# A hybrid SGU and latent-attention trunk: rows scaled by their reciprocal norm on VectorE and turned by plain transposes, in place of products with a diagonal

## The chip, the cores and the metric

The kernel runs on one core of a Trainium2 chip. The metric is the device time of one execution in microseconds (us), as the median of several runs; the profile is of one execution. PE is TensorE, DVE is VectorE, ACT is ScalarE, POOL is GpSimd, SP is SyncE, whose queue issues nearly all loads.

## What is computed

Two layers over a residual stream x of 256 rows and 2048 columns, all float32. Each layer normalises the rows, modulates them by a scale and a shift that come from a condition vector c, runs a mixer, and adds the gated, normalised result:

```python
cond = jax.nn.silu(c)
for i in range(DEPTH):
    mod = cond @ ada_w[i] + ada_b[i]
    shift, scale, gate = jnp.split(mod, 3, axis=-1)
    h = rms_norm(x, pre_g[i]) * (1 + scale[:, None, :]) + shift[:, None, :]
    j = i // N_MIXERS
    if i % N_MIXERS == 0:
        y = sgu_mixer(h, sgu_w_in[j], sgu_norm_g[j], sgu_w_s[j], sgu_b_s[j], sgu_w_out[j])
    else:
        y = mla_mixer(h, mla_w_in[j], mla_q_norm_g[j], mla_kv_norm_g[j], mla_w_uq[j], mla_w_ukv[j], mla_w_out[j])
    x = x + gate[:, None, :] * rms_norm(y, post_g[i])
```

Layer 0's mixer projects h to 12288 columns (gelu, layer norm, a spatial product, a silu gate) and back; layer 1's is latent attention of 16 heads. The change concerns only how h is made: `rms_norm(x, ...)`, which multiplies each row of x by the reciprocal of its root mean square, and the turning of the rows, so that the columns of x lie on the partitions, as the projections need it.

## The kernel before

The 256 rows are two blocks (b = 0, 1) of 128 rows on the 128 partitions. Weights stream from HBM in granules of two row chunks of 128 by 512 columns (512 KB); each is split into a high part (a cast on ACT, L71) and a low part (a subtraction on DVE, L72), and a product is the sum of three: high by high, high by low, low by high. A granule makes 12 such 128x512 matmuls, 6 for each block.

**What sets the order.** The class `Stream` (L60) holds two lists: loads, and stages (splits of granules, and hooks for other work). `get` runs the stages until the splits are a few granules (2 to 4) ahead of the products; a load is issued on SP when its stage comes within `RAW_BUFS` = 6 items. The queues of all engines keep the order in which the program issues, so a hook stands in an engine's queue where the stream put it. `spread(main, extra)` (L134) lays the items of `extra` evenly between those of `main`: here adaLN's items (load, multiply and sum `ada_w`, L289; sums over the partitions on PE, L301; L309 to L313 give shift and scale) and the steps that turn h, between weight granules.

**Layer 0.** x lies in tiles `xn[b][q]`, 128 rows by 512 columns, q = 0 to 3. `norm_x` (L525) forms each row's reciprocal root mean square on DVE and makes a diagonal of it, `dg0[b]`, tile `dx` (`diag_of`, L264, a multiplication of the identity). `turn_hT(k)` (L428) turns two column chunks, k and k + 1, of both blocks by four products of x with the diagonal into a PSUM bank `ht`: the product turns the rows and scales them at once. Then ACT applies scale and shift (`hf`, L458) and casts (`hH`, L461), and DVE makes the low part (`hL`, L465). This happens in eight turns, k = 0, 2, ..., 14. The first stands among the hooks at the start; the others come from `hT_steps` (L450), a list of steps in which turning, modulating and the low part of consecutive turns follow each other one step apart. `STEPS` (L30) says before which visit of the first projection each group is wanted. A visit (product `pi`) sums one 512-column chunk over the row chunks known so far into a PSUM bank; there are four such banks, and they are evacuated by ACT (L662) or added by DVE (L669) one step later.

**Between the layers.** `ready1` (L877) adds the residual to block b and takes the sums of squares; its last step makes the diagonal `dg1[b]` (tile `d`). The order in which the two layers interlock is written out by hand in `PLAN` (L53): T, F, H, L with two digits turn, modulate, cast, and make the low part of block b's quarter q; s splits a granule of weights, g and b are products of block 0 and of block 1 (`pm`), e and c are what is left of layer 0. `turn_h1` (L920) is T: four products with the diagonal into two PSUM banks `h`, and `mod_h1` is F, half on ACT, half on DVE.

Of the kernel before, what the change touches and what calls it, by code (L numbers as in the profile page):

```python
# [8 lines left out]
F32 = mybir.dt.float32  # L9
# [6 lines left out]
P = 128  # L16
# [12 lines left out]
# chunks of adaLN's rows: (first, number, the first projection's visit before which they come)  # L29
STEPS = ((0, 2, 0), (2, 2, 24), (4, 2, 45), (6, 2, 78), (8, 4, 115), (12, 4, 162))  # L30
# how far the splitting of weights runs ahead of their products, and where other work lies between them
# [19 lines left out]
# from layer 0 to layer 1: T, F, H, L turn, modulate and split block b's quarter q; g, b are products of block 0 and  # L51
# of block 1, s splits weights, c and e are what is left of layer 0
PLAN = "e1 e1 e1 e1 T00 T01 s1 F00 F01 H00 L00 H01 e1 e1 L01 T02 T03 g1 c1 F02 H02 c1 g1 g1 L02 s1 c1 c1 g1 c1 F03 c1 g1 H03 g1 L03 T11 s1 T10 F11 F10 H10 L10 g1 s1 b1 H11 b1 L11 T12 F12 H12 L12 s1 T13 b1 F13 H13 b1 b1 b1 L13 b1"  # L53
# buffers on chip
# [5 lines left out]
class Stream:  # L60
    """Weights on their way to TensorE: each item is loaded, then split into the two float32r parts, some steps
    before the products that take it. Other work that keeps step with the loads lies between the items."""
# [29 lines left out]
    def weights(self, name, src, rows=P, slot=None):  # L92
        """src: gk * rows rows, gn columns"""
# [41 lines left out]
def spread(main, extra):  # L135
    """the items of extra evenly between those of main"""
    if not main:
        return
    done = 0
    for i, m in enumerate(main):  # L140
        m()
        want = -(-len(extra) * (i + 1) // len(main))
        while done < want:
            extra[done]()
            done += 1
# [3 lines left out]
def tile_trunk(  # L149
# [114 lines left out]
    def diag_of(r, name):  # L264
        d = sp.tile([P, P], F32, tag="diag", name=name, bufs=4)
        nc.vector.tensor_scalar_mul(d, ident, r)
        return d

# [1 line left out]
    def ada_items(name, src, width, state):  # L270
        """src(k0, nk): the columns of nk row chunks, [P, nk, width] or with a pair of column ranges between"""
# [33 lines left out]
    def ada_put(l, k, n, ps_shift, ps_scale):  # L305
        """shift and scale of chunks k .. k + n from the sums"""
        ks = slice(k, k + n)
        i = l * 48 + k
        nc.vector.tensor_tensor(out=shift[:, l, ks], in0=ps_shift, in1=cols[:, 0, i:i + n], op=ALU.add)  # L309
        t = small(f"sc_{l}_{k}", n)  # L310
        nc.vector.tensor_tensor(out=t, in0=ps_scale, in1=cols[:, 0, i + 16:i + 16 + n], op=ALU.add)
        g = 96 + l * 16 + k
        nc.vector.scalar_tensor_tensor(amul[:, l, ks], t, 1.0, cols[:, 0, g:g + n], op0=ALU.add, op1=ALU.mult)  # L313
# [8 lines left out]
    def ada_range(l, k0, nk):  # L322
        """shift and scale of nk column chunks"""
# [7 lines left out]
    def ada_gate(l):  # L331
        """gate times post_g, as columns"""
# [20 lines left out]
    def spread_gate(l):  # L353
        """the gate as rows on all partitions, by way of a row in DRAM"""
# [36 lines left out]
    def chain(*fns):  # L391
        """the first now, each of the others one step later"""
        fns[0]()
        if len(fns) > 1:
            deferred.append(lambda: chain(*fns[1:]))

    def chunk_tasks(name, ks, lhs, evac, per=2):
        """one 512-column chunk of a product: tasks for both blocks, one pair for each granule of the weights"""
# [26 lines left out]
    # normalised, modulated rows turned for TensorE  # L425
    turned = {}

    def turn_hT(k):  # L428
        ps = turned[k] = aux_bank(f"ht_{k}")
        for i in range(2):  # L430
            for b in range(NB):
                src = xn[b][(k + i) // 4][:, ((k + i) % 4) * P:((k + i) % 4 + 1) * P]
                mm(ps[:, i * 256 + b * P:i * 256 + (b + 1) * P], src, dg0[b], True, True)
# [16 lines left out]
    def hT_steps(k0, nk):  # L450
        """the same in steps that lie apart, each engine's part on its own"""
# [16 lines left out]
        lists = [[lambda k=k: turn_hT(k) for k in ks], [lambda k=k: mod(k) for k in ks], [lambda k=k: low(k) for k in ks]]  # L468
        steps = []
        for i in range(len(ks) + 2):  # L470
            steps.append([lists[j][i - j] for j in (2, 1, 0) if 0 <= i - j < len(ks)])
# [8 lines left out]
    hH, hL = [None] * 8, [None] * 8  # L480
    dg0 = [None, None]
# [6 lines left out]
    # the first projection's cells: row chunks of h taken as their shift and scale come  # L488
# [36 lines left out]
    def norm_x():  # L525
        for b in range(NB):
            t = small(f"ssxt_{b}", 1)
            nc.vector.reduce_sum(out=t, in_=ssx[b], axis=AX.X)
            dg0[b] = diag_of(rstd_of(t, D, f"rx_{b}"), f"dx_{b}")

    # the first two chunks' shift and scale, on the way to the first product: TensorE takes a part of the rows itself
# [18 lines left out]
    def first_split():  # L550
        """the first weights' parts row chunk by row chunk, each as the products need it"""
# [82 lines left out]
    def fills(z, a, b):  # L634
        """what lies between the steps of a pair of heads, and what is left for after the last"""
# [237 lines left out]
    dg1 = [None, None]  # L873
# [3 lines left out]
    def ready1(b, gate):  # L877
# [10 lines left out]
        def turn():  # L888
            t = small(f"ss1t_{b}", 1)
            nc.vector.reduce_sum(out=t, in_=ss1, axis=AX.X)  # L890
            dg1[b] = diag_of(rstd_of(t, D, f"r1_{b}"), f"d1_{b}")
# [28 lines left out]
    def turn_h1(b, q):  # L920
        ps = hp1[b][q] = [aux_bank(f"h1_{b}_{q}_{i}") for i in range(2)]
        for i in range(4):
            mm(ps[i // 2][:, (i % 2) * P:(i % 2 + 1) * P], x1[b][q][:, i * P:(i + 1) * P], dg1[b], True, True)
# [44 lines left out]
    def go(n):  # L968
        """the next n granules' products of block 0"""
# [88 lines left out]
    # shared rope keys, once above zeros and once below, for the heads of a pair  # L1058
# [337 lines left out]
```

## Time and profile before

| | |
|---|---|
| median of 3 runs | 1158.54 us (1157.86 to 1158.56) |
| span of the profiled execution | 1157.2 us |
| PE busy | 1132.1 us (98%) |
| DVE busy | 892.2 us (77%) |
| ACT busy | 566.8 us (49%) |
| read from HBM | 300.39 MB, 261 GB/s over the span |

The profiled execution's own whole time is not on its page; the span runs from its first to its last instruction. Busy time is an average over stages with different limits. The idle time of an engine carries a releaser: what ended the wait. The chain is followed back from the last instruction, at each step to what released it; 87% of it lies on PE.

### The profile page before, as it was taken

How to read it: one execution, taken by the hardware profiler on the slowest of the kernel's cores; microseconds unless marked ns; L12 is line 12 of the kernel's file. 1: busy time of each engine (PE TensorE's matmuls, PEld its weight loads, DVE VectorE, ACT ScalarE, POOL GpSimd, SP SyncE). 2: the span in 40 equal slices, each digit the busy share in tenths (PEclk: the TensorE clock that was granted, in tenths of full speed). 3: DMA queues.
4: the chain of work that ended last, by engine and by line, in shares of the span. 5: the costliest groups of instructions: out<-in, count | busy, mean ns of one | idle time of the engine just before them, and what ended most of it. 6: DMA issues, size and time to landing. Idle time of an engine off the chain costs nothing.

```text
span 1157.2 us, 15835 instructions
## 1 busy us (share of the span) xinstructions
PE 1132.1 (98%) x5705; PEld 958.9 (83%) x5705; DVE 892.2 (77%) x1187; ACT 566.8 (49%) x811; POOL 20.4 (2%) x46
## 2 busy tenths in 40 slices
PE   5999999999999999999999999999999999999997
PEld 5788878888888888888888888888888989999885
DVE  4889898978987887888787878668777557558655
ACT  3764334354546655545443444456554445445541
POOL 1000000000000000000001000000000000000000
PEclk9999999999999999999999999999999999999999
DMA  9999898978887886888689999954988245245672
GB/s 317 328 322 321 273 364 290 370 254 277 298 293 232 288 272 230 280 272 284 226 315 371 356 318 373 360 175 148 342 310 293 61 136 166 68 145 183 226 271 86
DMA packets 157855, 303.57 MB, mean 262 GB/s; under 512 B 11961, under 2 KB 28960, under 8 KB 157776
## 3 DMA queue, kind: packets, MB, share of 16 engines
q1 hardware_dynamic: 155808, 297.05, 75.0%
q0 software_dynamic: 1936, 5.49, 1.7%
q8 instruction: 45, 0.74, 0.3%
q14 instruction: 34, 0.28, 0.1%
q10 hardware_dynamic: 32, 0.01, 0.0%
HBM read 300.39 MB, written 2.11 MB: 261 GB/s over the span
## 4 chain that ended last, share of the span: by engine, by line
PE 87%; DMA 4%; DVE 4%; ACT 2%; issue 2%; SPq 0%; DVEq 0%; ACTq 0%
PE pi L185 23%; PE piz L185 15%; PE po L185 15%; PE pm L185 11%; PE pp L185 8%; PE qn L185 3%; DMA wi<-in_sgu_w_in_dram 2%; PE k L185 2%; PE v L185 2%; PE s L185 2%; PE o L185 1%; PE qr L185 1%; PE pada L301 1%; PE mix L185 1%; DMA first<-in_ada_w_dram 1%
## 5 line engine op out<-in xcount | busy, mean ns | idle before, releaser
L289 DVE SCALAR_TENSOR_TENSOR acc_ada<-ada,sc,acc_ada 128x1024 f32<-128x1024 f32 (+1 forms) x135 | 148.6, 1100 | 1.1 <-DMA ada<-in_ada_w_dram 0.2
L289 DVE SCALAR_TENSOR_TENSOR acc_gate<-gate,sc,acc_gate 128x1024 f32<-128x1024 f32 x60 | 76.6, 1277 | 0.6 <-DMA gate<-in_ada_w_dram 0.6
L669 DVE TENSOR_TENSOR part<-pi,part 128x512 f32<-128x512 f32 x92 | 59.6, 682 | 4.8 <-PE pi L185 4.7
L71 ACT CAST wi_6h<-wi 128x1024 fp32r<-128x1024 f32 x24 | 25.1, 1051 | 42.3 <-DMA wi<-in_sgu_w_in_dram 35.8
L71 ACT CAST wi_8h<-wi 128x1024 fp32r<-128x1024 f32 x24 | 25.2, 1050 | 27.8 <-DMA wi<-in_sgu_w_in_dram 18.2
L71 ACT CAST wi_4h<-wi 128x1024 fp32r<-128x1024 f32 x24 | 25.2, 1050 | 27.5 <-DMA wi<-in_sgu_w_in_dram 24.3
L72 DVE TENSOR_TENSOR wi_10l<-wi,wi_10h 128x1024 fp32r<-128x1024 f32 x24 | 29.3, 1219 | 6.8 <-ACT wi_10h L71 6.8
L72 DVE TENSOR_TENSOR wi_12l<-wi,wi_12h 128x1024 fp32r<-128x1024 f32 x24 | 29.2, 1217 | 5.2 <-ACT wi_12h L71 5.2
L72 DVE TENSOR_TENSOR wi_6l<-wi,wi_6h 128x1024 fp32r<-128x1024 f32 x24 | 29.2, 1218 | 4.9 <-ACT wi_6h L71 4.9
L72 DVE TENSOR_TENSOR wi_14l<-wi,wi_14h 128x1024 fp32r<-128x1024 f32 x24 | 29.3, 1220 | 4.6 <-ACT wi_14h L71 4.6
L72 DVE TENSOR_TENSOR wi_8l<-wi,wi_8h 128x1024 fp32r<-128x1024 f32 x24 | 29.3, 1219 | 2.8 <-ACT wi_8h L71 2.5
L72 DVE TENSOR_TENSOR wi_4l<-wi,wi_4h 128x1024 fp32r<-128x1024 f32 x24 | 29.2, 1218 | 2.8 <-ACT wi_4h L71 2.7
L71 ACT CAST wi_2h<-wi 128x1024 fp32r<-128x1024 f32 x24 | 25.2, 1051 | 11.9 <-DMA wi<-in_sgu_w_in_dram 11.4
L72 DVE TENSOR_TENSOR wi_0l<-wi,wi_0h 128x1024 fp32r<-128x1024 f32 x23 | 28.1, 1221 | 3.3 <-ACT wi_0h L71 3.3
L1240 ACT ACTIVATE sm<-sm,nm 128x128 f32<-128x128 f32 (+1 forms) x32 | 14.3, 449 | 32.4 <-DVE nm L1238 32.4
L72 DVE TENSOR_TENSOR wi_2l<-wi,wi_2h 128x1024 fp32r<-128x1024 f32 x24 | 29.3, 1219 | 1.2 <-ACT wi_2h L71 1.1
L71 ACT CAST wi_0h<-wi 128x1024 fp32r<-128x1024 f32 x23 | 24.0, 1051 | 12.5 <-DMA wi<-in_sgu_w_in_dram 12.5
L71 ACT CAST wi_10h<-wi 128x1024 fp32r<-128x1024 f32 x24 | 25.1, 1045 | 10.0 <-DMA wi<-in_sgu_w_in_dram 7.7
L71 ACT CAST wi_14h<-wi 128x1024 fp32r<-128x1024 f32 x24 | 25.1, 1045 | 7.0 <-DMA wi<-in_sgu_w_in_dram 4.6
L71 ACT CAST wi_12h<-wi 128x1024 fp32r<-128x1024 f32 x24 | 25.1, 1048 | 5.0 <-PE pi L185 3.3
L185 PE MATMUL pi<-wi_4h,hH 128*128 128x512 f32 x64 | 25.3, 395 | 1.4 <-DVE part L669 1.4
L763 DVE SCALAR_TENSOR_TENSOR part<-mix,cols,part 128x256 f32<-128x256 f32 x32 | 13.3, 477 | 16.4 <-PE mix L185 16.4
(682 smaller groups left out, 3827.3 us busy)
## 6 DMA issues: line engine op xcount, KB each, us to landing
wi<-in_sgu_w_in_dram SPq DMA_DIRECT2D x191, 512.0 KB, 5.4
ada<-in_ada_w_dram SPq DMA_DIRECT2D x240, 256.0 KB, 5.2
gate<-in_ada_w_dram SPq DMA_DIRECT2D x64, 512.0 KB, 5.4
wo<-in_sgu_w_out_dram SPq DMA_DIRECT2D x64, 512.0 KB, 5.9
wm<-in_mla_w_in_dram SPq DMA_DIRECT2D x48, 512.0 KB, 5.6
wp<-in_mla_w_out_dram SPq DMA_DIRECT2D x32, 512.0 KB, 5.2
ukv<-in_mla_w_ukv_dram SPq DMA_DIRECT2D x16, 512.0 KB, 4.7
uq<-in_mla_w_uq_dram SPq DMA_DIRECT2D x12, 384.0 KB, 3.3
```

Of the source, the lines that this page charges most:

```text
L71: self.nc.scalar.copy(out=h, in_=src)
L72: self.nc.vector.tensor_tensor(out=l, in0=src, in1=h.bitcast(F32), op=ALU.subtract)
L185: nc.tensor.matmul(o, lhsT=l, rhs=r, start=start, stop=stop)
L289: nc.vector.scalar_tensor_tensor(acc, raw, w, acc, op0=ALU.mult, op1=ALU.add)
L301: nc.tensor.matmul(ps[:, j:j + 1], lhsT=state["acc"][:, j * P:(j + 1) * P], rhs=ones[:, 0:1], start=True, stop=True)
L669: nc.vector.tensor_tensor(out=part[n, b], in0=ps, in1=part[n, b], op=ALU.add)
L763: nc.vector.scalar_tensor_tensor(u[:, cs], ps[:, cs], bs_col(2 * j + i), u[:, cs], op0=ALU.add, op1=ALU.mult)
L1240: nc.scalar.activation(sm[:, i, :], sm[:, i, :], AF.Exp, bias=nm[:, i:i + 1], scale=scale, accum_out=su[:, i:i + 1])
```

## The change

In layer 0, `norm_x` keeps the reciprocal `rx[b]` itself and multiplies the first quarter of x by it in place (`scale_x(0)`); `hT_steps` gets a fourth list of steps, one step ahead of the turning, which scales the next quarter when its first chunk is due. `turn_hT` becomes plain transposes with the identity. In layer 1, `turn_h1` multiplies its quarter of x1 by `r1[b]` on DVE into a new tile `x1n`, and then transposes it. The remaining lines of the diff rename or drop the diagonals, or are comments.

```diff
-    def diag_of(r, name):
-        d = sp.tile([P, P], F32, tag="diag", name=name, bufs=4)
-        nc.vector.tensor_scalar_mul(d, ident, r)
-        return d
...
+    def scale_x(q):
+        for b in range(NB):
+            nc.vector.tensor_scalar_mul(xn[b][q], xn[b][q], rx[b])
...
-                mm(ps[:, i * 256 + b * P:i * 256 + (b + 1) * P], src, dg0[b], True, True)
+                nc.tensor.transpose(out=ps[:, i * 256 + b * P:i * 256 + (b + 1) * P], in_=src, identity=ident)
...
-        lists = [[lambda k=k: turn_hT(k) for k in ks], [lambda k=k: mod(k) for k in ks], [lambda k=k: low(k) for k in ks]]
+        lists = [[lambda k=k: scale_x(k // 4) if k % 4 == 0 else None for k in ks], [lambda k=k: turn_hT(k) for k in ks],
+                 [lambda k=k: mod(k) for k in ks], [lambda k=k: low(k) for k in ks]]
         steps = []
-        for i in range(len(ks) + 2):
-            steps.append([lists[j][i - j] for j in (2, 1, 0) if 0 <= i - j < len(ks)])
+        for i in range(len(ks) + 3):
+            steps.append([lists[j][i - j] for j in (3, 2, 1, 0) if 0 <= i - j < len(ks)])
...
-            dg0[b] = diag_of(rstd_of(t, D, f"rx_{b}"), f"dx_{b}")
+            rx[b] = rstd_of(t, D, f"rx_{b}")
+        scale_x(0)
...
-            dg1[b] = diag_of(rstd_of(t, D, f"r1_{b}"), f"d1_{b}")
+            r1[b] = rstd_of(t, D, f"r1_{b}")
...
+        x1n = slot(f"x1n_{b}_{q}")
+        nc.vector.tensor_scalar_mul(x1n, x1[b][q], r1[b])
         for i in range(4):
-            mm(ps[i // 2][:, (i % 2) * P:(i % 2 + 1) * P], x1[b][q][:, i * P:(i + 1) * P], dg1[b], True, True)
+            nc.tensor.transpose(out=ps[i // 2][:, (i % 2) * P:(i % 2 + 1) * P], in_=x1n[:, i * P:(i + 1) * P],
+                                identity=ident)
```

The change also moves instructions. SP's queue at the start, before and then after: `wi` is a granule of the first projection's weights, `ada` a pair of adaLN's loads for the second turn.

```order
L86 DMA wi_0_0_183<-in_sgu_w_in_dram 128x2x512
L86 DMA ada_2_0_193<-in_ada_w_dram 128x2x256 x2
L86 DMA wi_0_0_201<-in_sgu_w_in_dram 128x2x512
L86 DMA ada_2_2_228<-in_ada_w_dram 128x2x256 x2
L86 DMA wi_0_0_231<-in_sgu_w_in_dram 128x2x512
L86 DMA ada_2_4_235<-in_ada_w_dram 128x2x256 x2
```

```order
L86 DMA wi_0_0_183<-in_sgu_w_in_dram 128x2x512
L86 DMA ada_2_0_193<-in_ada_w_dram 128x2x256 x2
L86 DMA ada_2_2_201<-in_ada_w_dram 128x2x256 x2
L86 DMA wi_0_0_227<-in_sgu_w_in_dram 128x2x512
L86 DMA ada_2_4_229<-in_ada_w_dram 128x2x256 x2
L86 DMA wi_0_0_234<-in_sgu_w_in_dram 128x2x512
```

From the second on, each weight granule now stands one adaLN pair further back.

DVE's queue around the third turn of layer 0 (k = 4), before and then after: `amul` is the last of shift and scale for that turn, `wi_2_2l` are low parts of weights, `hL` is the low part of the turned h.

```order
L313 SCALAR_TENSOR_TENSOR amul<-sc_4_801,cols 128x2
L72 TENSOR_TENSOR wi_2_2l<-wi_2_2_733,wi_2_2h 128x1024
L72 TENSOR_TENSOR wi_2_2l<-wi_2_2_737,wi_2_2h 128x1024
L465 TENSOR_TENSOR hL_845<-hf_840,hH_843 128x512
L72 TENSOR_TENSOR wi_2_2l<-wi_2_2_761,wi_2_2h 128x1024
```

```order
L308 SCALAR_TENSOR_TENSOR amul<-sc_4_799,cols 128x2
L72 TENSOR_TENSOR wi_2_2l<-wi_2_2_716,wi_2_2h 128x1024
L425 TENSOR_SCALAR x_1_130<-x_1_130,rx_0i 128x512
L425 TENSOR_SCALAR x_1_138<-x_1_138,rx_1i 128x512
L72 TENSOR_TENSOR wi_2_2l<-wi_2_2_735,wi_2_2h 128x1024
L464 TENSOR_TENSOR hL_845<-hf_840,hH_843 128x512
L72 TENSOR_TENSOR wi_2_2l<-wi_2_2_738,wi_2_2h 128x1024
```

The two scales of x's second quarter now stand behind one of the splits and ahead of the next; PE's turn of that quarter stands right behind adaLN's sums, as before.

DVE's queue at the end of block 1's share of the layer change, before and then after: `h1f` is DVE's half of F, `h1L` is L, `wm` are layer 1's weights, `x1n` the scaled quarter.

```order
L72 TENSOR_TENSOR wm_14l<-wm_14_6555,wm_14h 128x1024
L948 TENSOR_TENSOR h1L_1_6883<-h1f_1_0_6837,h1H_1_6874 128x256
L948 TENSOR_TENSOR h1L_1_6883<-h1f_1_1_6838,h1H_1_6874 128x256
L935 TENSOR_SCALAR h1f_2_1_6893<-h_1_2_1_6887,amul,shift 128x128 x2
L948 TENSOR_TENSOR h1L_2_6901<-h1f_2_0_6892,h1H_2_6898 128x256
L948 TENSOR_TENSOR h1L_2_6901<-h1f_2_1_6893,h1H_2_6898 128x256
L72 TENSOR_TENSOR wm_0l<-wm_0_6571,wm_0h 128x1024
L935 TENSOR_SCALAR h1f_3_1_6923<-h_1_3_1_6911,amul,shift 128x128 x2
```

```order
L72 TENSOR_TENSOR wm_14l<-wm_14_6559,wm_14h 128x1024
L952 TENSOR_TENSOR h1L_1_6895<-h1f_1_0_6849,h1H_1_6886 128x256
L952 TENSOR_TENSOR h1L_1_6895<-h1f_1_1_6850,h1H_1_6886 128x256
L924 TENSOR_SCALAR x1n_2_6900<-yg_2_1_6315,r_1i 128x512
L939 TENSOR_SCALAR h1f_2_1_6907<-h_1_2_1_6899,amul,shift 128x128 x2
L952 TENSOR_TENSOR h1L_2_6915<-h1f_2_0_6906,h1H_2_6912 128x256
L952 TENSOR_TENSOR h1L_2_6915<-h1f_2_1_6907,h1H_2_6912 128x256
L72 TENSOR_TENSOR wm_0l<-wm_0_6575,wm_0h 128x1024
L924 TENSOR_SCALAR x1n_3_6926<-yg_3_1_6718,r_1i 128x512
L939 TENSOR_SCALAR h1f_3_1_6939<-h_1_3_1_6925,amul,shift 128x128 x2
```

A scale now stands ahead of each F of block 1, the one for quarter 3 behind the low part of quarter 2 and the split of `wm_0`. On PE the turns of quarters 2 and 3 follow each other directly, as before, and products of block 1 follow them.

## Rows read from the trace of the kernel before

**Rows 1.** The page: span, and part 1: busy us (share) xinstructions.

```profile
span 1157.2 us, 15835 instructions
...
PE 1132.1 (98%) x5705; PEld 958.9 (83%) x5705; DVE 892.2 (77%) x1187; ACT 566.8 (49%) x811; POOL 20.4 (2%) x46
```

**Rows 2.** Stretches: busy us of PE, PEld, DVE, ACT, POOL; PEclk, DMA, GB/s.

```profile
150.00:185.00 35.00, 33.57 (x162) 27.91 (x161) 31.85 (x36) 14.87 (x16) 0.00 (x0) 1.00 1.01 361
...
770.00:800.00 30.00, 29.50 (x161) 24.79 (x160) 22.01 (x51) 22.55 (x57) 0.63 (x2) 1.00 0.23 71
```

**Rows 3.** Timeline of PE: start us, us, what, [idle before <-releaser].

```profile
42.66 0.50 PE L185 MATMUL pi<-wi_0h,hH 128*128 128x512 f32 x1 [1.11 <-ACT part L662]
...
99.38 0.50 PE L185 MATMUL pi<-wi_2h,hH 128*128 128x512 f32 x1 [0.38 <-DVE part L669]
...
171.02 0.47 PE L185 MATMUL pi<-wi_4h,hH 128*128 128x512 f32 x1 [1.43 <-DVE part L669]
```

**Rows 4.** The chain: start us, us, what (ht, yt, h: turned tiles).

```profile
57.86 0.90 PE ht L185 x8
...
170.19 0.69 DVE part L669
...
428.65 0.87 PE yt L801 x8
...
773.78 1.80 PE h L185 x16
```

**Rows 5.** The tile yt: duration ns min/median/max, first and last start us, forms.

```profile
L801 PE MATMUL yt<-ident,part x64: 270/273/273, 428.5 to 601.8; 128*128 128x128 f32 x64
```

**Rows 6.** Timeline of DVE: a 128x512 multiplication, and layer 1's first diagonal.

```profile
4.46 0.49 DVE L540 TENSOR_SCALAR acc_first<-first,sc 128x512 f32<-128x512 f32 x1 [3.45 <-DMA first<-in_ada_w_dram]
...
773.18 0.29 DVE L266 TENSOR_SCALAR d<-ident,r_0i 128x128 f32<-128x128 f32 x1
```

**Rows 7.** Timeline at the start: DVE, the DMA queue of SP, ACT.

```profile
22.48 3.10 DVE L542 SCALAR_TENSOR_TENSOR acc_first<-first,sc,acc_first 128x512 f32<-128x512 f32 x4
...
34.79 0.42 SPq L86 DMA_DIRECT2D wi<-in_sgu_w_in_dram  x1
35.96 0.88 SPq L86 DMA_DIRECT2D ada<-in_ada_w_dram  x2
...
41.08 1.05 ACT L71 CAST wi_0h<-wi 128x1024 fp32r<-128x1024 f32 x1 [2.40 <-DMA wi<-in_sgu_w_in_dram]
```

**Rows 8.** Timeline around the third turn of layer 0: DVE, then PE.

```profile
84.86 2.48 DVE L72 TENSOR_TENSOR wi_2l<-wi,wi_2h 128x1024 fp32r<-128x1024 f32 x2
...
84.25 1.14 PE L185 MATMUL ht<-dx,x 128*128 128x128 f32 x8
85.14 0.48 PE L185 MATMUL pi<-wi_0h,hH 128*128 128x512 f32 x1
```

**Rows 9.** Timeline before the fifth turn: DVE, then PE.

```profile
179.93 1.28 DVE L669 TENSOR_TENSOR part<-pi,part 128x512 f32<-128x512 f32 x2
...
181.13 1.05 PE L185 MATMUL ht<-dx,x 128*128 128x128 f32 x8
```

**Rows 10.** Timeline at the change of layers: DVE, ACT, PE.

```profile
789.60 1.23 DVE L72 TENSOR_TENSOR wm_12l<-wm,wm_12h 128x1024 fp32r<-128x1024 f32 x1 [0.40 <-ACT wm_12h L71]
...
794.67 0.75 DVE L948 TENSOR_TENSOR h1L<-h1f,h1H 128x256 fp32r<-128x256 f32 x2
...
798.38 1.23 DVE L72 TENSOR_TENSOR wm_0l<-wm,wm_0h 128x1024 fp32r<-128x1024 f32 x1 [0.53 <-ACT wm_0h L71]
...
797.30 1.05 ACT L71 CAST wm_0h<-wm 128x1024 fp32r<-128x1024 f32 x1
...
790.40 0.48 PE L185 MATMUL pm<-wm_12h,h1H 128*128 128x512 f32 x1
...
795.13 1.95 PE L185 MATMUL h<-d,yg 128*128 128x128 f32 x16
796.83 0.48 PE L185 MATMUL pm<-wm_4h,h1H 128*128 128x512 f32 x1
```

More of the change, by code (lines that the diff above doesn't have):

```diff
@@ L480, in tile_trunk @@
     hH, hL = [None] * 8, [None] * 8
-    dg0 = [None, None]
+    rx = [None, None]
     def w_chunk(name, w, k0, nk, n, slots=()):
@@ L872, in tile_trunk @@
     x1 = yg[0]
-    dg1 = [None, None]
+    r1 = [None, None]
     later = []
```

## The prediction

> **What bounds the kernel now.** I read the page first, then TensorE's idle time in the timeline, then the stretches, then the places that the change touches. TensorE (PE) is busy 98% of the span [rows 1], and its clock was granted in full in the stretches that the change touches [rows 2]. So a microsecond taken off PE counts, wherever PE is what everybody waits for. The reader should see where that is not so. Between 30 us and 185 us PE stands still three times, each time for an evacuation by ScalarE (ACT) or VectorE (DVE) of a PSUM bank [rows 3]. The evacuation is late because it stands behind the splitting of weights in its engine's queue, and that waits for loads: from 150 to 185 us the DMA share is 1.01 and DVE is busy 31.85 of 35 us [rows 2]. There PE follows the other engines. From 171 us to the change of layers (773 us) PE never waits. From 770 to 800 us the DMA has almost nothing to do (0.23), and PE, DVE and ACT hand small tiles to each other; PE idles only 0.5 us of it [rows 2]. Both of the change's places, `turn_hT` and `turn_h1`, lie in these two delicate stretches.
>
> **What the change removes on PE.** A turn of layer 0 is 4 products with a diagonal, recorded as 8 passes, 0.90 us; layer 1's 8 products took 1.80 us, so 225 ns each. Plain transposes of the same shape are in the trace (`yt`): 8 in 0.87 us, so 109 ns each, one record each [rows 4]. A turn of 4 should take 0.435 us and save 0.46 us; the 64 instructions together save 7.4 us of PE time.
>
> A page speaks against this. A record of `yt` lasts 273 ns, twice the pitch, because neighbours overlap [rows 5]. The Trainium skill (TensorE: Matmul & The Clock Gate, Part 4: PE-mode transpose) gives about 275 ns for a transpose in a kernel's context; the record's length agrees, the pitch here does not. Paid in a row at that price, a turn of 4 would cost 1.10 us, 0.20 us more than the products. The sum goes by the pitch.
>
> **What it adds on DVE.** Out go four diagonals of 0.29 us. In come 16 multiplications of 128x512 f32 from SBUF to SBUF. The first `acc_first` is the same form and took 0.49 us [rows 6]. Two of them in a row are taken as 0.9 us, a little under 2 x 0.49, since neighbours on DVE overlap slightly (the evacuation `part` takes 0.69 us alone, two take 1.28, [rows 4, 9]). DVE grows by 16 x 0.49 - 4 x 0.29 = 6.7 us. What matters is which of them PE now waits for: the products needed a diagonal made long before, while every transpose needs a scaled tile, and the scale stands in DVE's queue right before the turn, behind splits that wait for ACT.
>
> **The start (to 43 us).** DVE's four `acc_first` run without a gap and PE waits for the last [rows 7]. Two diagonals (0.57 us) go from ahead of them and two scales (0.97 us) come: +0.4 us. Then the order of loads: `hT_steps` has one step more, so the even spreading of adaLN's items among the weights puts each weight load behind one more adaLN load. ACT casts the fifth weight tile at 41.08 us, as soon as it lands, and the bank that PE waits for until 42.66 us is evacuated right behind that cast [rows 3, 7]. Its load was issued at 34.79 us; in the new order it takes the place of the adaLN load at 35.96 us [rows 7]. So +1.2 +0.4 = +1.6 us at 42.66 us. The first turn is hidden behind `acc_first`, the second (57.9 us) saves 0.46: PE is +1.1 us late, DVE some +0.6 us.
>
> **Third turn (84 us).** Here tile x_1 is scaled for the first time. In DVE's new order the scales come behind a weight split: the first of the pair at 84.86 us ends near 86.05, the scales end near 86.95, and with 0.15 us of hand-over (DVE's `part` ends at 170.19 + 0.69, PE starts at 171.02) the turn can start at 87.1 instead of 84.25 us [rows 3, 4, 8]. With DVE's own +0.6, PE goes on at 87.7 + 0.44 instead of 85.14 us [rows 8]: +3.0 us. PE's earlier +1.1 is swallowed by this wait. The stall at 99.38 us gives back 0.38 [rows 3], the fourth turn (128 us) saves 0.46: +2.15 us. The chain to the stall at 171 us starts from that turn (ACT cannot cast on before it), so I carry +2.15 through, with both ends kept: 0, if DVE and DMA make it up, and +3.
>
> **Turns five to eight.** Before the fifth, x_2 is scaled behind two evacuations that DVE ends at 181.2 us, while PE reaches the turn at 181.13 us [rows 9]: scales until 182.05, PE +1.0 us. Less 2 x 0.46: +0.1. The last two are moved one weight tile later and x_3 is scaled well ahead, in a gap of DVE: -0.92. So far +1.35 us.
>
> **The change of layers (773 to 802 us).** Block 0's first scales stand where the diagonal stood at 773.18 us [rows 6]; four turns are 1.86 us shorter, but each pair waits for its scales, and about 0.4 us are left when block 1's norm is ready. In block 1 the order T11, split, T10, ..., T12, ..., split, T13 decides. Before, T11 and T10 needed one diagonal, T12 and T13 none. Now x1n for T10 stands behind the split of wm_12 (it waits for its cast; 789.60 us, now 0.4 earlier): split to 790.4, scale to 790.85, hand-over, T10 turned near 791.45. The next product starts 1.05 us later than 790.40 [rows 10]. DVE then lags by some 0.3 us: the low part of quarter 1, that ended at 794.67 + 0.75 = 795.4, ends near 795.75. The scale for T12 is done near 796.2, so T12 starts at 796.35 instead of 795.13 us. T13's scale stands behind DVE's share of F12, the low part L12 and the split of wm_0, and that split waits for a cast that ACT does after its own F12 and H12. Before, the split ended at 798.38 + 1.23 = 799.6 us [rows 10]; now T12 starts 1.2 us later and takes 0.46 less, so the split ends 0.75 later, at 800.35, the scale at 800.8, and T13 is turned from 800.95 to 801.4 us. PE's queue is in order: the products behind T13, ready long before, started at 796.83 us [rows 10]. So +4.6 us here, waits and savings in. The cast of wm_0 (797.30 us before) ends last ahead of that split, so it sets the bounds: 3.6, if it comes a microsecond sooner; 5.6, if later. Nothing behind gives it back: the timeline has no idle time of PE from 793 to 928 us.
>
> **Sum.** 1.35 + 4.6 = +5.95 us on the profiled execution's span of 1157.2 us [rows 1]: 1163.15. Its own whole time is not on the page; the median of the runs, 1158.54, lies 1.34 us over the span. With that unchanged, 1164.5 us, 0.5% slower. What a measurement of this kernel can tell from no change is 0.2%, 2.3 us.
>
> **The rivals.**
> - *The early delay is made up* (DVE and DMA reach the stall at 171 us when they did before): 4.6 + 0.1 - 0.92 = +3.8, 1162.3 us. For it: PE's own wait at 171 us was 1.43 us [rows 3], so PE was ahead of the others there. Against: the chain there starts at a turn.
> - *Scales ready in time, so faster.* If every scale but the first were ready when PE comes, 60 instructions x 0.116 us would count: 1158.5 - 7.0 = 1151.6 us. It decides at T13: its scale would have to be done by 795.6 us, but the cast that the split ahead of it needs started at 797.30 us [rows 10]. Against it, plainly.
> - *The waits are half as long* (ACT and DVE run ahead at the layer change, third turn near its old time): about +1.5, 1160.0 us, no measurable change.
> - *The loaded stretch multiplies delays:* the reordered loads cost again at 100 to 171 us, bounds of the layer change high: +9.5, 1168.0 us. Against it: after 171 us PE never waited.
> - *Transposes at 0.27 us in a row,* as records that don't overlap [rows 5]: six turns x 0.66 us, and about 1 us more at the layer change: 1169.5 us. It is the page's price; `yt` speaks against it [rows 4].
>
> **How the numbers follow.** Forecast 0.60; early delay made up 0.17; faster 0.05; half the waits 0.09; multiplied delays 0.07; slow transposes 0.02. Faster by over 0.2%: 0.05. Within: 0.09. Slower: 0.86. The forecast's bounds (3.6 to 5.6 at the layer change, 0 to 3 early) give 1161.3 to 1166.4; the range reaches a little into the neighbours on both sides: 1160.8 to 1167.4 us, which leaves out the faster case, most of the half waits and the slow tails.
>
> **What would show it.** Right: PE idle before T13 for about 4 us, released by a DVE multiplication, and before T12 and T10 for about 1 us; idle before the third turn of 2 to 3 us with the same releaser; a stall near 43 us longer than 1.1 us; 109 ns a transpose. Wrong: PE reaching T13 without a wait (the order on DVE would not be the order in time), a stall at 171 us that shrinks to nothing (the early delay made up), turns of 0.9 us or more (the transposes not cheaper), a granted clock below full after the longer waits.

## The result, and the profile after

The changed kernel takes 1171.24 us (median, 1168.94 to 1174.16) against 1158.55 us before: a ratio of 1.0108, with a 95% interval of 1.0096 to 1.0120. It is slower, as forecast, but by 12.7 us and not by 6, and outside the range. The profiled execution took 1174.16 us, span 1172.4 us, and is the longest of the four, so its numbers account for 15.2 us.

The page after, span and part 1, as in [rows 1]: PE has the same busy time in a span that is 15 us longer.

```profile
span 1172.4 us, 15718 instructions
...
PE 1132.4 (97%) x5641; PEld 954.4 (81%) x5641; DVE 897.8 (77%) x1199; ACT 567.3 (48%) x811; POOL 20.6 (2%) x46
```

Sixty-four fewer instructions and yet no less busy time: some of PE's instructions ran slower. The stretches show which (columns as in [rows 2]; the third number from the right is the granted clock). 1.00 is 2.4 GHz, 0.50 is 1.2 GHz, and values between them are means over the stretch:

```profile
85.00:90.00 5.00, 1.47 (x8) 1.42 (x8) 4.45 (x8) 4.06 (x5) 0.00 (x0) 0.71 1.00 339
90.00:95.00 5.00, 4.63 (x15) 3.77 (x16) 3.18 (x5) 3.36 (x5) 0.00 (x0) 0.60 0.97 348
630.00:635.00 5.00, 4.75 (x26) 3.82 (x26) 3.29 (x6) 2.12 (x3) 0.00 (x0) 0.83 1.04 381
635.00:640.00 5.00, 5.00 (x20) 4.06 (x19) 2.32 (x3) 2.01 (x2) 0.00 (x0) 0.83 1.05 385
805.00:810.00 5.00, 0.97 (x6) 0.76 (x5) 3.12 (x6) 2.49 (x6) 0.00 (x0) 0.74 0.27 93
810.00:815.00 5.00, 5.00 (x15) 3.99 (x14) 4.48 (x8) 3.43 (x6) 0.00 (x0) 0.58 0.51 147
```

Before, the clock stood at 1.00 where the program does the same work; two of the stretches of before, around the third turn and behind the turns of block 1:

```profile
85.00:90.00 5.00, 5.00 (x25) 4.17 (x24) 3.40 (x4) 4.95 (x8) 0.00 (x0) 1.00 1.08 364
795.00:800.00 5.00, 5.00 (x32) 4.44 (x31) 3.58 (x9) 3.65 (x8) 0.00 (x0) 1.00 0.36 105
```

Now it falls three times: at the third turn (85 to 95 us), near 633 us, where the change does nothing, and at T13, the turn of block 1's last quarter.

PE's timeline names the waits (columns as in [rows 3]); the first row answers to the row at 42.66 us there and the last, the same product in the order of the program, to the one at 171.02 us. The rows from 86.75 us on stand at the third turn:

```profile
44.57 0.50 PE L185 MATMUL pi<-wi_0h,hH 128*128 128x512 f32 x1 [1.22 <-ACT part L663]
...
86.75 1.47 PE L296 MATMUL pada<-ones,acc_ada 128*128 128x1 f32 x8 [2.09 <-DVE acc_ada L284]
90.37 1.21 PE L432 MATMUL ht<-ident,x 128*128 128x128 f32 x4 [2.15 <-DVE x L425]
91.23 0.78 PE L185 MATMUL pi<-wi_0h,hH 128*128 128x512 f32 x1
91.80 0.63 PE L185 MATMUL pi<-wi_0h,hL 128*128 128x512 f32 x1
92.23 0.63 PE L185 MATMUL pi<-wi_0l,hH 128*128 128x512 f32 x1
...
171.90 0.47 PE L185 MATMUL pi<-wi_4h,hH 128*128 128x512 f32 x1 [1.46 <-DVE part L670]
...
178.14 0.47 PE L185 MATMUL pi<-wi_4h,hH 128*128 128x512 f32 x1 [0.53 <-DVE part L670]
```

The reader should see two things. There are two waits in place of the forecast's one: 2.15 us for the scaled x, which was forecast, and ahead of it 2.09 us for `acc_ada`, adaLN's running sum. And behind them products start 0.43 us apart, where the same products start 0.23 us apart at full clock. The stall at 171.90 us is not the one at 171.02 us of before: its product ran at 163.98 us there and did not wait.

What `acc_ada` waited for stands in the timelines of ACT and DVE:

```profile
83.63 1.05 ACT L71 CAST wi_2h<-wi 128x1024 fp32r<-128x1024 f32 x1 [2.38 <-DMA wi<-in_sgu_w_in_dram]
...
84.71 1.23 DVE L72 TENSOR_TENSOR wi_2l<-wi,wi_2h 128x1024 fp32r<-128x1024 f32 x1 [1.59 <-ACT wi_2h L71]
85.86 0.74 DVE L284 SCALAR_TENSOR_TENSOR acc_ada<-ada,sc,acc_ada 128x512 f32<-128x512 f32 x1
...
88.26 0.16 DVE L304 TENSOR_TENSOR shift<-pada,cols 128x2 f32<-128x2 f32 x1 [0.52 <-PE pada L296]
...
88.60 1.23 DVE L72 TENSOR_TENSOR wi_2l<-wi,wi_2h 128x1024 fp32r<-128x1024 f32 x1
89.74 0.48 DVE L425 TENSOR_SCALAR x<-x,rx_0i 128x512 f32<-128x512 f32 x1
90.14 0.48 DVE L425 TENSOR_SCALAR x<-x,rx_1i 128x512 f32<-128x512 f32 x1
```

A weight's load came late, its cast waited 2.38 us for it, the split of that weight waited for the cast, and the sum stood behind the split in DVE's queue. Then DVE waited for PE's sums to make shift and scale, and the scales of x stood behind these and the next split. So a PE that comes late to the sums gets its scaled x late, too.

At the change of layers, PE's timeline has the four turns of block 1 (T11, T10, T12, T13) and the products behind the last; DVE's has what T13 waited for (it answers to [rows 10]):

```profile
797.41 0.66 PE L926 MATMUL h<-ident,x1n 128*128 128x128 f32 x4 [1.39 <-DVE x1n L924]
799.22 0.63 PE L926 MATMUL h<-ident,x1n 128*128 128x128 f32 x4 [1.15 <-DVE x1n L924]
...
804.56 0.66 PE L926 MATMUL h<-ident,x1n 128*128 128x128 f32 x4 [0.36 <-DVE x1n L924]
809.24 1.12 PE L926 MATMUL h<-ident,x1n 128*128 128x128 f32 x4 [4.03 <-DVE x1n L924]
810.01 0.78 PE L185 MATMUL pm<-wm_4h,h1H 128*128 128x512 f32 x1
810.59 0.63 PE L185 MATMUL pm<-wm_4h,h1L 128*128 128x512 f32 x1
```

```profile
807.57 1.23 DVE L72 TENSOR_TENSOR wm_0l<-wm,wm_0h 128x1024 fp32r<-128x1024 f32 x1 [0.49 <-ACT wm_0h L71]
808.71 0.48 DVE L924 TENSOR_SCALAR x1n<-yg,r_1i 128x512 f32<-128x512 f32 x1
```

The scale for T13 stands behind the split of `wm_0`, and PE stands still for 4.03 us. That is the forecast's mechanism. But the nine products behind T13 then start 0.43 us apart and not 0.23.

To see where the time is lost, one compares the start of the same product in two traces. From the views of the tiles `piz` and `pm` (duration min/median/max in ns, first to last start in us), first before, then after:

```profile
L185 PE MATMUL piz<-wi_0h,hL x32: 388/389/390, 398.6 to 575.2; 128*128 128x512 f32 x32
L185 PE MATMUL pm<-wm_0h,h1L x24: 387/389/499, 780.2 to 926.3; 128*128 128x512 f32 x24
```

```profile
L185 PE MATMUL piz<-wi_0h,hL x32: 389/389/389, 404.9 to 581.6; 128*128 128x512 f32 x32
L185 PE MATMUL pm<-wm_0h,h1L x24: 387/389/505, 787.9 to 941.4; 128*128 128x512 f32 x24
```

So PE is 6.3 us late when layer 0's turns are over (first `piz`, 398.6 us before) and 15.1 us late behind the change of layers (last `pm<-wm_0h,h1L`, 926.3 us before). The table of all kernels further down is read in this way.

### The profile page after: what moved, and what is told of

It is laid out like the page before. It is cut to its first block, busy times and chain, and to the rows that moved or that the text cites. A ratio compares the mean times of both kernels' runs of the same rounds, so it can differ in the third digit from the quotient of the medians.

```text
span 1172.4 us, 15718 instructions
## 1 busy us (share of the span) xinstructions
PE 1132.4 (97%) x5641; PEld 954.4 (81%) x5641; DVE 897.8 (77%) x1199; ACT 567.3 (48%) x811; POOL 20.6 (2%) x46
## 4 chain that ended last, share of the span: by engine, by line
PE 81%; DVE 7%; DMA 6%; issue 3%; ACT 3%; SPq 1%; DVEq 0%; ACTq 0%
PE pi L185 22%; PE piz L185 13%; PE po L185 12%; PE pm L185 10%; PE pp L185 7%; PE qn L185 2%; DMA wi<-in_sgu_w_in_dram 2%; PE k L185 2%; PE v L185 2%; PE s L185 2%; DMA wo<-in_sgu_w_out_dram 2%; DVE acc_ada L284 1%; PE o L185 1%; PE qr L185 1%; PE pada L296 1%
## 5 line engine op out<-in xcount | busy, mean ns | idle before, releaser
L185 PE MATMUL pi<-wi_0h,hH 128*128 128x512 f32 x60 | 24.6, 410 | 2.6 <-ACT part L663 2.6
```

Of the source, the lines that this page charges most:

```text
L185: nc.tensor.matmul(o, lhsT=l, rhs=r, start=start, stop=stop)
```

## The experiments

Theory A: the waits come as forecast, and what is missing is TensorE's clock, which falls in them and makes PE slow for some microseconds more. Theory B: in layer 0 it is the new order of the loads, which the forecast priced at 1.2 us, that costs the time. The first four runs take the change apart.

**Layer 1 alone** (the kernel before, with `turn_h1` changed and the reciprocal `r1[b]` kept in place of its diagonal):

```diff
+        x1n = slot(f"x1n_{b}_{q}")
+        nc.vector.tensor_scalar_mul(x1n, x1[b][q], r1[b])
...
-            mm(ps[i // 2][...], x1[b][q][...], dg1[b], True, True)
+            nc.tensor.transpose(out=ps[i // 2][...], in_=x1n[...], identity=ident)
```

> The kernel before with the change in layer 1 alone (scaled quarters x1n, transposes); layer 0 keeps its products with a diagonal. In the trace of the changed kernel the layer change costs 6.8 us (PE's delay against before grows from 8.4 us in the middle of the last output column to 15.2 us after it). Theory A (the waits that were forecast come, and in the longest of them TensorE's clock falls to its lower level, which costs some 2.5 us more than the wait): a wait of about 4 us ahead of T13, a granted clock of 0.50 behind it, 1158.5 + 6.8 = 1165.3 us. Theory B (the layer change costs what the forecast said, 4.6 us, and the rest of it was carried over from layer 0's delay): 1163.1 us and no fall of the clock.

Measured: 1165.97 us, ratio 1.0062 (1.0047 to 1.0077), so +6.9 us. T13 in PE's timeline, and the stretches around T10 and T13:

```profile
801.72 1.11 PE L925 MATMUL h<-ident,x1n 128*128 128x128 f32 x4 [4.03 <-DVE x1n L923]
```

```profile
790.00:795.00 5.00, 4.05 (x13) 3.46 (x14) 3.73 (x9) 3.55 (x9) 0.00 (x0) 0.66 0.34 105
800.00:805.00 5.00, 3.28 (x11) 2.81 (x12) 3.63 (x7) 2.53 (x7) 0.00 (x0) 0.66 0.36 108
```

The 4.03 us wait is there without any of layer 0's delay, and so is the fall of the clock. Theory B falls for the layer change. The clock falls here behind T11's and T10's waits of 1.36 and 1.15 us as well (790 to 795 us); in the changed kernel waits of 1.39 and 1.15 us at the same turns left it at 1.00.

**Layer 0 alone** (the changed kernel, with `turn_h1` and its diagonal as before):

```diff
-            r1[b] = rstd_of(t, D, f"r1_{b}")
+            dg1[b] = diag_of(rstd_of(t, D, f"r1_{b}"), f"d1_{b}")
...
-        x1n = slot(f"x1n_{b}_{q}")
-        nc.vector.tensor_scalar_mul(x1n, x1[b][q], r1[b])
...
+            mm(ps[i // 2][...], x1[b][q][...], dg1[b], True, True)
```

> The kernel before with the change in layer 0 alone (x scaled in place a step ahead, transposes, one step more among the loads); layer 1 keeps its diagonal. In the trace of the changed kernel PE is 6.4 us late from 270 to 620 us, 8.4 us after a fall of the clock near 632 us. Theory A: waits of about 2 us each ahead of adaLN's sums and the third turn, then the lower clock until about 94 us: 1158.5 + 6.4 = 1164.9 us, and 1166.9 if the fall near 632 us comes too. Theory B (no part of it is the clock's, the waits come and go): 1158.5 + 1.4 (the forecast) = 1159.9 us.

Measured: 1163.48 us, ratio 1.0035 (1.0020 to 1.0049), so +4.4 us. This lies between the two expectations. The wait for the scaled x is 2.15 us here too, that for `acc_ada` 0.40 us and not 2.09, for the same instructions: when the weight's load lands differs from one execution to the next. The fall near 632 us does not come, but another does, behind adaLN's sums for the fifth turn:

```profile
180.00:185.00 5.00, 5.00 (x18) 4.01 (x18) 4.96 (x10) 2.09 (x2) 0.00 (x0) 0.66 0.99 345
```

**The empty step alone** (the kernel before, its loads and turns in the changed kernel's order; no scaling, diagonals everywhere):

```diff
-        lists = [[lambda k=k: turn_hT(k) for k in ks], [lambda k=k: mod(k) for k in ks], ...]
+        lists = [[lambda: None for k in ks], [lambda k=k: turn_hT(k) for k in ks], ...]
...
```

> The kernel before with nothing but an empty step ahead of the turns of layer 0, so that loads and turns stand in the changed kernel's order; products with diagonals in both layers, no scaling. Theory A with the scales as the cause of the early loss: only the start's +1.2 us and small changes: 1159.7 us, and PE does not wait 2 us near 85 us. Rival (the order of the loads is the cause): PE waits some 2 us ahead of adaLN's sums for the third turn, for a weight's cast that waits for its load: 1158.5 + 1.4 + 2.1 = 1162 us, and 1164.5 if the clock falls there without any scale.

Measured: 1163.94 us, ratio 1.0041 (1.0026 to 1.0056), so +4.8 us, without one scale or transpose. PE's timeline, and the stretch behind the second row:

```profile
44.09 0.50 PE L185 MATMUL pi<-wi_0h,hH 128*128 128x512 f32 x1 [1.31 <-ACT part L663]
...
85.84 1.02 PE L301 MATMUL pada<-ones,acc_ada 128*128 128x1 f32 x8 [1.06 <-DVE acc_ada L289]
```

```profile
85.00:90.00 5.00, 4.16 (x20) 3.90 (x21) 4.14 (x8) 3.97 (x5) 0.00 (x0) 0.69 1.05 379
```

So the empty step, which moves the loads and sets the turns one granule later, costs by itself as much as the whole change of layer 0, with a fall of the clock and no scale at all. The rival of this run is right. In layer 0 alone the transposes save some 3 us besides (next run), so by subtraction the late scales cost about as much again. The wait for `acc_ada` is not the moved loads' alone: it is 0.73 us in the run with layer 1 alone, whose layer 0 is as before.

**The transposes alone** (the changed kernel without its scales and without the additional step):

```diff
-        scale_x(0)
...
-        nc.vector.tensor_scalar_mul(x1n, x1[b][q], r1[b])
...
-            nc.tensor.transpose(out=..., in_=x1n[:, i * P:(i + 1) * P], identity=ident)
+            nc.tensor.transpose(out=..., in_=x1[b][q][:, i * P:(i + 1) * P], identity=ident)
```

> The changed kernel without any scaling of rows (neither x in layer 0 nor x1 in layer 1 is multiplied by its reciprocal norm), and with the loads in the order of before: the plain transposes alone. If a transpose costs 109 ns in a row, 64 of them save 7.4 us of PE time; 0.46 us (first turn) are hidden and some 1.4 us are swallowed by the stalls near 99 and 171 us: 1158.5 - 5.5 = 1153 us, no fall of the clock. Rival (transposes cost their record's 0.27 us in a row, or the clock falls because of them): 1158.5 us or more.

Measured: 1154.37 us, ratio 0.9960 (0.9945 to 0.9975), so -4.7 us. The transposes are as cheap as `yt` said: a gain of 3.2 us in layer 0 and of 0.8 us in layer 1, where PE, now sooner, waits 1.07 us for ACT's cast of `wm_12` and 0.52 us for its low part. Behind these waits the clock falls, which was not expected (a mean of 0.68 from 785 to 790 us), and takes a part of layer 1's gain.

The next run asks whether the clock's fall costs what theory A says, by adding work to PE:

```diff
+    def pe_fill(bank, n):
+        for _ in range(n):
+            mm(bank[:, 0:P], ident, ident, True, True)
...
+        if name == "pada_0_4":
+            pe_fill(ps, 4)
...
+        if k == 4:
+            pe_fill(ps, 9)
...
+        pe_fill(ps[0], {(1, 1): 5, (1, 0): 4, (1, 3): 16}.get((b, q), 0))
```

> The changed kernel with more work for PE and nothing else: products of the identity with itself (0.225 us each, into the PSUM bank that is filled right behind them) stand where PE waited in the changed kernel: 4 ahead of adaLN's sums for the third turn, 9 ahead of the third turn, 5 ahead of T11, 4 ahead of T10, 16 ahead of T13. They last 0.9, 2.0, 1.1, 0.9 and 3.6 us, each a little less than the wait that it fills. Theory A (the waits let TensorE's clock fall, and that costs 3 us at the third turn and 2.5 us at T13 beside the waits): the granted clock stays at 1.00 at both places and the kernel gets faster by the added work, 1171.2 - 5.5 = 1165.7 us. Rival (the clock falls for another reason, or its fall is hidden): 1171 us or more.

Measured: 1166.01 us, ratio 1.0059 (1.0044 to 1.0074): 38 more products, 8.6 us of work, and 5.2 us less time than the changed kernel. Two stretches, and in PE's timeline T13 with the filling ahead of it:

```profile
85.00:90.00 5.00, 4.93 (x42) 4.53 (x41) 4.69 (x9) 3.33 (x5) 0.00 (x0) 1.00 1.03 354
...
800.00:805.00 5.00, 4.55 (x33) 4.05 (x32) 3.43 (x8) 2.79 (x7) 0.00 (x0) 1.00 0.33 91
```

```profile
798.54 3.74 PE L185 MATMUL h<-ident 128*128 128x128 f32 x32
802.73 0.66 PE L935 MATMUL h<-ident,x1n 128*128 128x128 f32 x4 [0.45 <-DVE x1n L933]
803.14 0.48 PE L185 MATMUL pm<-wm_4h,h1H 128*128 128x512 f32 x1
```

Less PE's delay ahead of the change of layers, T13 comes as late as in the changed kernel (802.73 - 2.0 and 809.24 - 8.4 us), but PE goes on at full clock. So at T13 theory A is shown. At the third turn the two executions differ in one thing more: `acc_ada` is ready at 85.32 us here and at 86.60 us in the changed kernel, and nothing that was added stands ahead of it. How the 5.2 us divide was asked with the filling in layer 0 alone (the last line of the diff left out):

```diff
-        pe_fill(ps[0], {(1, 1): 5, (1, 0): 4, (1, 3): 16}.get((b, q), 0))
```

> The changed kernel with the products of the identity in layer 0 alone: 4 ahead of adaLN's sums for the third turn, 9 ahead of that turn; nothing added at the change of layers, so that the 4 us wait ahead of T13 and the clock's fall behind it stay. What is open is how the 5.2 us that the products in both layers gave back (1171.24 to 1166.01 us) divide. If they divide as PE's delays in the traces do (2.4 us at the change of layers, the rest early): 1168.4 us. Rival (as with the empty step alone, where the fall of the clock near 87 us was made up later by the stalls at 99 and 171 us, so that all of the gain came from T13): 1170.7 us or more.

Measured: 1168.45 us, ratio 1.0076 (1.0062 to 1.0090). So by the medians 2.8 us are layer 0's and 2.4 us those of the change of layers. The traces agree on the second: over the change of layers PE's delay grows by 6.6 us here and by 4.3 us with the filling there too. For the first, the run with layer 0 alone is the nearer trace, since `acc_ada` is ready at 84.03 us there and at 83.83 us here: from 69.7 to 92.7 us PE's delay grows by 1.4 us less with the waits filled. The rest of the 2.8 us is not traced to a cause.

If theory A and the place of the scales explain the loss, scales that are issued early, with the loads as before, must turn the change into a gain. In layer 0 the additional step goes, and the quarters 1 to 3 go to places that were empty:

```diff
             apart = [lambda: None] * APART
-            spread(todo, items[:-1] + apart + items[-1:] + apart + hT_steps(...))
+            q = {2: 1, 6: 2, 12: 3}.get(STEPS[si][0])
+            first = apart if q is None else [lambda q=q: ST.hook(lambda: scale_x(q))]
+            spread(todo, items[:-1] + first + items[-1:] + apart + hT_steps(...))
```

> Layer 0 with scaled rows and plain transposes, but without the additional step: the loads and turns keep the order of the kernel before, and x's quarters 1, 2 and 3 are scaled in places that were empty ahead of adaLN's sums for chunks 2, 6 and 12, some 25 to 50 us ahead of their first turn (quarter 0 as in the changed kernel). Layer 1 with its diagonal. Theory (the moved loads made layer 0's loss of 4.5 us, as the run with the empty step alone had it, and the transposes save what they should): some 2.5 us faster than before, 1156.6 us, no wait of PE at the turns. Rival (the scales on DVE cost in this stretch whatever their place, through the splits behind them): 1159 to 1161 us.

Measured: 1156.94 us, ratio 0.9982 (0.9973 to 0.9992). The third turn in PE's timeline, now with nothing ahead of it:

```profile
83.63 0.63 PE L437 MATMUL ht<-ident,x 128*128 128x128 f32 x4
84.02 0.47 PE L185 MATMUL pi<-wi_0h,hH 128*128 128x512 f32 x1
```

In layer 1, N is the scale as a step of its own in `PLAN`:

```diff
-PLAN = "... T00 T01 s1 ... g1 L03 T11 s1 T10 F11 ... L10 g1 s1 b1 H11 b1 L11 T12 ..."
+PLAN = "... N00 T00 N01 T01 N02 N03 s1 ... g1 N11 L03 T11 N10 s1 T10 F11 ... L10 N12 g1 s1 b1 H11 b1 L11 N13 T12 ..."
```

> Layer 1 alone changed, with the scales of its quarters issued ahead of the splits on DVE: block 0's quarters 2 and 3 right behind 0 and 1, block 1's quarter 1 ahead of the low part of block 0's quarter 3, quarter 0 right behind it ahead of the split of wm_12, quarter 2 behind the low part of quarter 0, quarter 3 behind that of quarter 1. Theory (T13's and T10's waits came from the place of the scales behind splits): no 4 us wait ahead of T13, 1.15 us ahead of T10 gone, 1158.8 us (the run without scaling gained only 0.8 us here, and 0.5 us of waits are new). Rival (DVE's added work alone delays the splits and PE as much): 1163 to 1166 us.

Measured: 1157.73 us, ratio 0.9988 (0.9979 to 0.9998), 8.2 us less than layer 1 alone with its scales late, for the same instructions. PE's turns of block 1:

```profile
787.72 0.66 PE L929 MATMUL h<-ident,x1n 128*128 128x128 f32 x4 [1.58 <-DVE x1n L924]
788.88 0.63 PE L929 MATMUL h<-ident,x1n 128*128 128x128 f32 x4 [0.50 <-DVE x1n L924]
...
794.17 0.60 PE L929 MATMUL h<-ident,x1n 128*128 128x128 f32 x4
794.92 0.66 PE L929 MATMUL h<-ident,x1n 128*128 128x128 f32 x4 [0.15 <-DVE x1n L924]
```

T13 waits 0.15 us in place of 4.03, T10 0.50 in place of 1.15; T11 waits 1.58 us. Both of these edits in one kernel (no further edit):

> Both layers with scaled rows and plain transposes, loads in the order of before, all scales early as in the two kernels ahead of this one. If the two add up: 1156.6 + 1158.8 - 1159.1 = 1156.3 us, faster than before by 2.8 us and faster than the changed kernel by 15 us. Rival (scales cost wherever they stand): 1163 us or more.

Measured: 1156.02 us, ratio 0.9974 (0.9965 to 0.9983): 3.1 us under the kernel before and 15.2 us under the changed one. The two gains (2.2 and 1.4 us) add up to 3.6; the 0.5 us between are less than the intervals resolve. In its trace the clock falls to a mean of 0.66 from 785 to 790 us, behind a wait of 1.58 us for T11's scale; in the run before this one the same wait left it at 1.00. To see what that fall costs, six products of the identity were put there:

```diff
+        for _ in range(6 if (b, q) == (1, 1) else 0):
+            mm(ps[0][:, 0:P], ident, ident, True, True)
```

> The kernel with both layers' scales early and the loads in the order of before, and 6 products of the identity with itself (1.35 us) ahead of T11, where PE waited 1.58 us and its clock then fell to 0.66 between 785 and 790 us. Theory (that fall costs 1.3 to 1.7 us): 1154.6 us. Rival (the fall comes from the narrow transposes that follow, and comes all the same, or is covered by a later wait): 1156.0 us.

Measured: 1156.08 us, ratio 0.9970 (0.9959 to 0.9981): no difference, although the clock in that stretch is now 1.00. By PE's delays the layer change gains 0.5 us, less than these intervals resolve; the expectation of 1.3 to 1.7 us was wrong.

Two runs on the moved loads remain. The first puts the empty step behind the turns, so that the loads keep the new order and the turns come as early as before:

```diff
+        steps.append([])
```

> As the run with the empty step alone (products with diagonals, no scaling), but with the empty step behind the turns of each group and not ahead of them: the loads are interleaved in the same new order, while turning, modulating and low part follow adaLN's sums at the distance of before. Theory (the new order of the loads is the cause: it delays weights, casts and evacuations): 1163.5 us, waits near 40 and 44 us and ahead of adaLN's sums near 85 us as there. Rival (the loss came from turning one weight granule later): 1159 to 1160 us.

Measured: 1168.80 us, ratio 1.0080 (1.0066 to 1.0094). It is not the later turn that costs: with the loads in the new order and the turns early the loss doubles, to +9.6 us, which neither side expected. PE waits 2.47 us for `acc_ada` at 87.91 us and 1.75 and 1.49 us for evacuations at 165.91 and 173.08 us. The clock falls here too, to a mean of 0.66 from 90 to 95 us. Why it is worse than with the turns late was not tried.

The second fills the wait ahead of adaLN's sums in the kernel with the empty step alone:

```diff
+        for _ in range(4 if name == "pada_0_4" else 0):
+            mm(ps[:, 0:P], ident, ident, True, True)
```

> As the run with the empty step alone, and 4 products of the identity with itself (0.9 us) ahead of adaLN's sums for the third turn, where PE waited 1.06 us and its clock then fell to 0.50 from 87 to 91 us. Theory (some 2 us of that run's loss are the clock's, the rest the loads'): 1161.9 us and a clock of 1.00. Rival (the loss is all of the loads, the clock's fall is made up later by the stalls at 99 and 171 us): 1163.9 us.

Measured: 1164.10 us, ratio 1.0039 (1.0026 to 1.0052). The clock stays at 1.00, and nothing is gained: here the rival holds. PE is 1.7 us less late behind the third turn (2.4 and 4.1 us at 92.7 us), and the later stalls take all but 0.4 us of that.

PE's delay against the trace of before, in us, at five products (their starts before: `pi<-wi_2h,hL` first 69.7, `pi<-wi_2h,hH` 20th 92.7, `piz<-wi_0h,hL` first 398.6, `po<-wo_0h,yL` last 733.2, `pm<-wm_0h,h1L` last 926.3); the kernels are one execution each. Their starts differ by up to 0.5 us, and two executions of the same layer 0 (both early, with and without products that keep PE busy later) lie 1.5 us apart at 398.6:

| kernel | 69.7 | 92.7 | 398.6 | 733.2 | 926.3 | median, us |
|---|---|---|---|---|---|---|
| changed | +1.4 | +7.4 | +6.3 | +8.4 | +15.1 | 1171.24 |
| layer 1 alone | -0.3 | +0.3 | +0.1 | +0.2 | +6.6 | 1165.97 |
| layer 0 alone | +0.5 | +4.5 | +4.5 | +4.5 | +4.4 | 1163.48 |
| empty step alone | +1.5 | +4.1 | +4.5 | +4.6 | +4.5 | 1163.94 |
| empty step, PE busy | +1.3 | +2.4 | +4.1 | +4.1 | +4.0 | 1164.10 |
| empty step last | +2.2 | +6.2 | +8.7 | +8.7 | +8.6 | 1168.80 |
| no scaling | -1.2 | -1.3 | -3.2 | -3.1 | -3.9 | 1154.37 |
| changed, PE busy in both | +1.8 | +4.3 | +2.0 | +2.0 | +6.3 | 1166.01 |
| changed, PE busy in layer 0 | +0.5 | +3.1 | +2.2 | +2.2 | +8.7 | 1168.45 |
| layer 0, early scales | -1.1 | -1.1 | -2.6 | -2.6 | -2.7 | 1156.94 |
| layer 1, early scales | -0.5 | -0.2 | -0.5 | -0.5 | -1.5 | 1157.73 |
| both early | -1.1 | -1.0 | -2.6 | -2.6 | -3.1 | 1156.02 |
| both early, PE busy | -0.4 | -0.4 | -1.1 | -1.1 | -2.2 | 1156.08 |

## Why the prediction was wrong

The sign and most of the waits held; two terms and so the size did not. Step by step:

- *What the transposes save.* Right. A turn of 4 and the hand-over to the next product take 0.35 us where nothing waits (59.56 to 59.91 us), against 0.435 forecast. The run without scaling is 4.7 us faster. A record of `yt` lasts 273 ns [rows 5], near the 275 ns that the Trainium skill (TensorE: Matmul & The Clock Gate, Part 4: PE-mode transpose) gives, but neighbours overlap, so that length is not the price of a transpose in a row.

```profile
59.56 0.60 PE L432 MATMUL ht<-ident,x 128*128 128x128 f32 x4
59.91 0.48 PE L185 MATMUL pi<-wi_0h,hH 128*128 128x512 f32 x1
```

- *The start.* Right: the stall moved from 42.66 to 44.57 us (+1.9, forecast +1.6), and PE is 1.4 us late behind the second turn (forecast +1.1).
- *The third turn.* Half right. The wait for the scaled x is 2.15 us (forecast 2.85). The 2.09 us ahead of adaLN's sums were not in the forecast, because it applied the new order of the loads only to the first five weights, though it stands in every group. This is the mis-sized term: 1.2 us for the moved loads, where the empty step, which moves them, costs 4.8 us by itself. Nor is PE's earlier delay of 1.1 us "swallowed by this wait": the scales stand behind work of DVE that waits for PE's own sums (0.52 us, at 88.26 us), so the delay is carried on. At 92.7 us PE is 7.4 us late, against 3.0 forecast.
- *Turns five to eight.* That the delay is carried through the stall at 171 us was right, not its size: the product that started at 171.02 us starts at 178.14, so 7.1 us late against 2.15 forecast. The fifth turn waits 0.17 us, not 1.0. With PE kept busy, layer 0 ends 2.0 to 2.2 us late, against 1.35 forecast; as the moved loads cost more than was forecast, that is in part luck.
- *The change of layers.* T10 waits 1.15 us (forecast 1.05), T13 4.03 us (about 4), T12 0.36 (some 1 us), T11 1.39 us (not forecast). With PE kept busy the layer change costs 6.3 - 2.0 = 4.3 us, against 4.6 forecast.
- *The step that failed* is the one that is missing: a wait was priced at its length. In the changed kernel TensorE's clock falls in the waits of 2 and 4 us, and the work behind them runs at half rate; 5.2 us of the 6.7 us that the forecast lacked came back when PE was kept busy, 2.4 us of them at the change of layers, where T13 comes no sooner, and 2.8 us in layer 0, where a pair of traces with equal loads shows 1.4 us. The prediction named "a granted clock below full after the longer waits" as a sign that it was wrong, and gave it no price and no chance. The kernel kept busy takes 1166.0 us, inside the range.

The trace of before shows such a fall behind PE's last work:

```profile
1145.00:1150.00 5.00, 3.70 (x17) 2.73 (x15) 2.87 (x6) 0.98 (x3) 0.00 (x0) 1.00 0.62 210
1150.00:1155.00 5.00, 0.00 (x0) 0.00 (x0) 3.21 (x7) 0.00 (x1) 0.00 (x0) 0.68 0.61 203
```

PE stands still, and the mean clock of the next 5 us is 0.68. The Trainium skill (TensorE: Matmul & The Clock Gate, Part 1: The HAM clock gate) says that the clock falls to half when PE idles, and these rows agree. With a wait of 4 us in the forecast, the two rows asked for a term.

Of the rivals, *multiplied delays* (1168.0 us, a chance of 0.07) came nearest in number, with the loads as its first cause, but it placed their cost at 100 to 171 us, and PE is no later at the product of 171.02 us (7.1 us) than at 92.7 us (7.4 us); *scales ready in time* was wrong for this kernel and right as a remedy: 1156.02 us.

## What to carry to other kernels

A product that scales and turns at once takes its factor long before; a scale ahead of a plain transpose puts the whole queue of another engine between data and PE, so issue it ahead of the splits and casts that wait, and the same instructions go from +6.9 to -1.4 us. A wait on TensorE can have two prices, its length and the lower clock behind it (2.4 us behind the wait of 4.03 us here); work of no use in the wait tells them apart. A step that does nothing is not free where loads are laid evenly between steps: it cost 4.8 us here, and 9.6 us with the turns left where they were.

## What the runs showed of the hardware

The clock fell where waits were not the longest: in the run with the empty step behind a wait of 1.06 us that eight one-column products followed, and in the profiled execution of the changed kernel near 633 us, behind a wait of 0.25 us and sixteen one-column products (PE's delay grew by 2.0 us there, which no other trace shows). It fell also with layer 0 alone near 181 us, behind sixteen one-column products. In the trace of before, a wait of 1.43 us left it at 1.00. And the same wait at the same instructions can do either: T11's wait of 1.58 us left it at 1.00 in the run with layer 1's early scales and is followed by a mean of 0.66 in the run with both. So a trace without a fall does not show that a wait is free of one. What tells these apart the runs do not show. Nor does a fall always cost: at 87 us in the run with the empty step later stalls covered it, at T13 nothing did.
